# A trunk layer with routed experts: the first gather in one product, four more weight chunks ahead, and a reordered end with row pairs added by GpSimd

## The chip, the cores and the metric

The kernel runs on one core of one Trainium2 chip. The metric is device time in microseconds (us), the median of several executions. A profile is one further execution, recorded instruction by instruction. Engine names as the profile has them: PE is TensorE's matmul, PEld its weight load, DVE is VectorE, ACT is ScalarE, POOL is GpSimd, and SP is SyncE, which here only issues transfers (SPq in the rows).

## The reference, cut to what matters

One layer over 512 tokens of 1024 channels, all in float32. An attention part (two branches, gates, an output projection, a LayerNorm) makes `h`. Then each token picks one group of experts and two experts in that group:

```python
x = _layer_norm(ALPHA * x + mixed, ln1_g, ln1_b)          # h, 512 x 1024
g_val, g_idx = lax.top_k(softmax(x @ w_group + b_group), 1)
top_val, top_idx = lax.top_k(e_logits_of_that_group, 2)
combine = ...                                               # weight of each token in each of 32 experts
for g in range(4):                                          # 8 experts of width 256 in each group
    hid = silu(x @ w_gate[g]) * (x @ w_up[g]) * combine[:, g]
    y = y + hid @ w_down[g]
return _layer_norm(ALPHA * x + y, ln2_g, ln2_b)
```

## The kernel before

**Stages.** Up to about 345 us the kernel projects and attends; to 401 us it multiplies by the output matrix, tile by tile (four tiles of 128 tokens, two halves of 512 columns), adds the residual into `hp[tt]`, normalizes and routes; to 420 us it gathers the rows of the first four experts; then come 32 experts, and from about 646 us on the closing sums, the second LayerNorm and the output.

**Precision.** Exact float32 products are made in two ways: a float32 operand in one product, or a rounded part (type fp32r) and the remainder in two quicker products. `split` makes the two parts: ACT rounds, and DVE or POOL subtracts. `split_h` (line 837) does so for the normalized tile: DVE scales and shifts each half of `hp[tt]` (line 848), ACT writes `hh` (line 112), POOL writes `hl` (line 115), and then the tile goes to DRAM (`hD<-hp`, line 853), from where later experts fetch their rows by index.

**First gather.** The rows of experts 0 to 3 (64 each, so 256) are not fetched but multiplied out: `gathered` (line 995) multiplies `hh[tt]` and `hl[tt]` by a one-hot matrix `onehot` (256 columns) for each of 8 channel blocks and 4 tiles, into eight banks called `trf`. What can be done while the last tiles are routed is done there (table `TAIL`, with some idle products between); tile 3, and blocks 6 and 7, come last, in `prep_first`. `onehot` of tile 3 stands at the end of DVE's routing chain (lines 894 to 929).

**Weights.** The experts' 192 chunks (`we`, 128 x 1024 floats, 512 KB each) are loaded in a fixed order by SP, which waits in order, instruction by instruction. Chunk i goes into a buffer of one of four pools (`RING`: 0 is `slots`, 1 is `slots2`, 2 `hip`, 3 `lop`), 43 buffers in one round. 13 chunks are loaded from inside the output projection (`EARLY`, `EARLY_AT`), five of them into `slots2`; all others are issued from the experts' loop, up to 47 ahead of use, when a buffer comes free. `slots2` has 15 buffers, and also holds `hp`, `hh`, `hl` and the first LayerNorm's gain and bias.

**Experts.** For each expert: `gate_up` (4 chunks, 16 products into `sc`), ACT and DVE join the two half sums into `gus`, four transposes (`stp`), ACT's silu and DVE's multiply (`sg`), then `down` (2 chunks, 8 products into `tr`). For experts 0 to 27 the weighted rows go to DRAM by index (`y2D`), two rows for each token. The last four experts ("late") don't: their rows are kept in SBUF as `late`, split in halves of columns into a rounded and a remainder part (lines 1199, 1204, 1206), and are added into the result by products with a selection matrix `stl`.

**The end.** The two stored rows of every token come back as `yy` (eight transfers of 512 KB, line 1251). Eight banks `fin0` to `fin7` (two for each tile) sum up: products of `late` with `stl` ("add") and products of `yy` with the identity ("rows"). Tiles 0 and 1 take both rows of a pair by products; for tiles 2 and 3 POOL adds the pair first (line 1290). The order is written out by hand in `FIN`. Then statistics, gain, scale and bias of each tile, on DVE, ACT and POOL, and the store.

Of the kernel before, what the change touches and what calls it, by code (L numbers as in the profile page):

```python
# [45 lines left out]
EARLY = 13  # L46
K2 = 5
EARLY_AT = (0, 0, 5)
# [20 lines left out]
H_POOL = (0, 1, 2, 3)  # L69
LATE_C = (2, 3)  # L70
H_STT = (0, 1, 2, 3)
# [9 lines left out]
Y_PE = (0, 1)  # L81
Y_POOL = (2, 3)
# [3 lines left out]
FIN_AT = {31: (0, 1, 2, 3)}  # L86
FIN = (
# [16 lines left out]
def trunk(ctx, tc, xT, x, wm, wv, wbr, wout, wr, br, bg, rbx, lnp, lncol, wexp, out):  # L104
# [726 lines left out]
    hh, hl = [None] * TT, [None] * TT  # L831
# [5 lines left out]
    def split_h(tt):  # L837

        r, mean = rs[tt]
        if tt in LATE_C:  # L840
            centre(tt, mean)
        t = slot([P, D], F32R, f"hh{tt}", slots2)
        lo = slot([P, D], F32R, f"hl{tt}", slots2)
        for k in range(2):
            cs = slice(k * S, (k + 1) * S)
            src = hp[tt][:, cs]
            if tt in H_STT:
                nc.vector.scalar_tensor_tensor(out=src, in0=src, scalar=r, in1=lnb[:, cs], op0=OP.mult, op1=OP.add)
# [197 lines left out]
    for tt in range(TT):  # L1046
        at = (0, tt + 1) if tt + 1 < TT else (1, 0)
        todo.setdefault((*at, PT[0]), []).extend([lambda tt=tt: turn(tt, 0), lambda tt=tt: first_half(tt)])
        todo.setdefault((*at, PT[1]), []).append(lambda tt=tt: run(lg[tt, 0]))
        todo.setdefault((1, tt + 1, PT[0]), []).extend([lambda tt=tt: turn(tt, 1), lambda tt=tt: begin(tt), lambda tt=tt: scale1(tt)])  # L1050
        todo.setdefault((1, tt + 1, PT[1]), []).extend([lambda tt=tt: choose(tt)])
        todo.setdefault((1, tt + 1 + PT[2] // 8, PT[2] % 8), []).append(lambda tt=tt: run(rt[tt]))
        todo.setdefault((1, tt + 1 + PT[3] // 8, PT[3] % 8), []).append(lambda tt=tt: split_h(tt))
# [18 lines left out]
    def load_early():  # L1072
        for _ in range(EARLY):
            raw_load()

    todo.setdefault(EARLY_AT, []).append(load_early)
# [102 lines left out]
    def down(e):  # L1179
        p, odd = e // 2, e % 2  # L1180
        is_late = p >= NPAIR - NLATE
        odd_last = p == NPAIR - 1
        if is_late:
            late.append(hip.tile([P, D], F32R, tag="hi", name=f"late{e}"))
        elif not odd:
            oe[p] = bp.tile([P, D], F32, tag="oe", name="oe", bufs=2)
        ps = pb.tile([P, 512], F32, tag="tr", name="tr", bufs=3)
        sides = [slice(half * CAP, (half + 1) * CAP) for half in range(2)]
# [4 lines left out]
        if is_late:  # L1193
            sums = slot([P, D], F32, f"sum{e}", slots2)
            cs = [slice(half * 512, half * 512 + 512) for half in range(2)]
            scs = [(wslot if half == odd else wswap)[sides[half], p : p + 1] for half in range(2)]
            for half, here in enumerate(sides):
                x = (xg if half == odd else xo)[p]
                pin(nc.vector.scalar_tensor_tensor(
                    out=sums[here, cs[half]], in0=ps[here], scalar=scs[half], in1=x[here, cs[half]],  # L1200
                    op0=OP.mult, op1=OP.add,
                ))
            for half, here in enumerate(sides):
                pin(nc.scalar.activation(late[-1][here, cs[half]], sums[here, cs[half]], AF.Copy))
            for half, here in enumerate(sides):
                pin((nc.gpsimd if half and odd_last else nc.vector).tensor_sub(
                    late[-1][sides[1 - half], cs[half]], sums[here, cs[half]], late[-1][here, cs[half]].bitcast(F32)
                ))
            return
        for half in (odd, 1 - odd):  # L1210
            cs = slice(half * 512, half * 512 + 512)
# [21 lines left out]
    late = []  # L1233
# [51 lines left out]

    def fin_sum(tt):
        a, b = y2[tt]
        if tt in Y_PE:
            return
        pin((nc.gpsimd if tt in Y_POOL else nc.vector).tensor_add(a, a, b))  # L1290

    def finish():

        for step in FIN:
# [3 lines left out]
            if what == "down":  # L1298
                down(tt)
# [4 lines left out]
            elif what == "sum":  # L1304
                fin_sum(tt)
            elif what == "rows":
                for n, t in enumerate(y2[tt] if tt in Y_PE else y2[tt][:1]):
                    fin_rows(tt, t, n == 1 or tt not in Y_PE)
# [42 lines left out]
    for e in range(NE):  # L1351
# [18 lines left out]
        act(e)  # L1370
# [131 lines left out]
```

## Time and profile before

| what | value |
|---|---|
| median of 3 executions | 679.63 us (677.06 to 679.9) |
| the profiled execution: its own time; the span of its instructions | 682.24 us; 680.4 us |
| PE busy; DVE; ACT; POOL | 640.9 us (94%); 408.2 us (60%); 322.6 us (47%); 105.1 us (15%) |
| transfers | 158.62 MB, mean 233 GB/s |
| mean granted clock of TensorE | 0.987 of full speed |

The page begins with the busy time of each engine; a busy PE is not PE at its peak, since products overlap. Then the span is cut in 40 slices of 17 us, each digit a share in tenths. The chain is followed back from the last instruction to what released each step. The views by stretch and by time used below give the same for chosen microseconds.

### The profile page before, as it was taken

What the parts mean: (1) busy time and instruction counts of PE and PEld (TensorE: products, weight loads), DVE (VectorE), ACT (ScalarE), POOL (GpSimd) and SP (SyncE); (2) the same over time, 40 slices, a digit from 0 to 9 for tenths busy, and PEclk for the clock granted to TensorE, in tenths of its full rate; (3) what the DMA queues carried; (4) which work ended last, traced back from release to release, by engine and by line L of the source; (5) the groups of instructions that cost most, each with busy time, mean ns of one, the idle gap of its engine ahead of it and who ended that gap; (6) DMA issues with size and microseconds to landing.
All of it is one profiled execution on the core that took longest, in us unless ns stands there. A gap on an engine that the chain in (4) does not pass through costs nothing.

```text
span 680.4 us, 8940 instructions
## 1 busy us (share of the span) xinstructions
PE 640.9 (94%) x3116; PEld 420.4 (62%) x3116; DVE 408.2 (60%) x836; ACT 322.6 (47%) x642; POOL 105.1 (15%) x152
## 2 busy tenths in 40 slices
PE   8999999999999999989999997899999988889894
PEld 4888878887878888878888775334343322224342
DVE  5676768678868877563674796234444433335466
ACT  5576877766656555744533232333322222222444
POOL 2012121101100110050000133121121111110044
PEclk8999999999999999999999998999999999999997
DMA  8600059203130323016794678999999999999943
GB/s 328 261 0 1 1 191 380 78 2 94 47 108 17 109 78 108 32 57 209 279 362 157 214 252 341 408 408 410 409 408 409 407 408 406 406 403 406 405 198 126
DMA packets 48032, 158.62 MB, mean 233 GB/s; under 512 B 7529, under 2 KB 7673, under 8 KB 47984
## 3 DMA queue, kind: packets, MB, share of 16 engines
q1 hardware_dynamic: 43632, 150.16, 58.2%
q0 software_dynamic: 4352, 7.85, 3.0%
q8 instruction: 26, 0.43, 0.3%
q14 instruction: 22, 0.18, 0.1%
HBM read 150.16 MB, written 15.73 MB: 244 GB/s over the span
## 4 chain that ended last, share of the span: by engine, by line
PE 52%; DMA 20%; DVE 15%; ACT 7%; issue 3%; POOL 0%; SPq 0%; DVEq 0%; POOLq 0%; ACTq 0%
DMA we<-in_wexp_dram 18%; PE pj L130 16%; PE sc L130 10%; PE pb L130 7%; PE po L130 4%; PE tr L130 4%; DVE t L482 3%; PE fin L130 2%; PE pv L130 2%; DVE wl L115 2%; PE av L130 2%; ACT wh L112 2%; DVE t L480 1%; PE tr L536 1%; DMA raw<-in_wm_dram 1%
## 5 line engine op out<-in xcount | busy, mean ns | idle before, releaser
L130 PE MATMUL sc<-we,xp 128*64 128x512 f32 x448 | 108.1, 604 | 7.4 <-DMA we<-in_wexp_dram 5.6
L130 PE MATMUL pj<-xh,wh 128*128 128x512 f32 x256 | 103.9, 406 | 1.7 <-ACT wh L112 1.6
L130 PE MATMUL pj<-xh,wl 128*128 128x512 f32 x256 | 101.2, 395 | 0.0
L130 PE MATMUL pj<-xl,wh 128*128 128x512 f32 x256 | 101.0, 394 | 0.0
L115 DVE TENSOR_TENSOR wl<-raw,wh 128x1024 fp32r<-128x1024 f32 (+1 forms) x57 | 69.9, 1230 | 23.0 <-ACT wh L112 22.8
L1152 DVE TENSOR_TENSOR gus<-gus,sc 64x512 f32<-64x512 f32 x32 | 21.7, 679 | 85.6 <-ACT gus L1151 83.5
L130 PE MATMUL tr<-we,sg 128*64 128x512 f32 x256 | 63.3, 601 | 5.3 <-DMA we<-in_wexp_dram 2.6
L112 ACT ACTIVATE wh<-raw 128x1024 fp32r<-128x1024 f32 (+1 forms) x57 | 58.7, 1037 | 18.7 <-DMA raw<-in_wbr_dram 4.7
L130 PEld LDWEIGHTS sc<-we,xp 128*64 128x64 f32 x448 | 27.4, 136 | 63.2 <-issue 33.1
L1151 ACT ACTIVATE gus<-sc 64x512 f32<-64x512 f32 x32 | 19.0, 593 | 88.6 <-PE sc L130 88.6
L130 PEld LDWEIGHTS pj<-xh,wh 128*128 128x128 f32 x256 | 48.6, 190 | 11.2 <-ACT wh L112 2.1
L130 PEld LDWEIGHTS pj<-xh,wl 128*128 128x128 f32 x256 | 48.5, 189 | 11.1 <-DVE wl L115 0.4
L130 PEld LDWEIGHTS pj<-xl,wh 128*128 128x128 f32 x256 | 48.6, 190 | 8.4
L130 PEld LDWEIGHTS tr<-we,sg 128*64 128x64 f32 x256 | 16.4, 136 | 44.9 <-issue 31.5
L130 PE MATMUL pb<-y,wh 128*128 128x512 f32 x128 | 40.0, 394 | 0.3 <-DVE k L345 0.3
L115 DVE TENSOR_TENSOR wl<-tr,wh 128x512 fp32r<-128x512 f32 (+1 forms) x64 | 30.9, 484 | 11.9 <-ACT wh L112 11.6
L1225 POOL DMA_INDIRECT y2D<-oe,rowi x14 | 14.0, 998 | 146.3 <-DVE oe L1216 120.2
L489 POOL TENSOR_SCALAR_AFFINE_SELECT w<-w 128x128 f32<-128x128 f32 x32 | 16.1, 514 | 126.2 <-ACT w L486 118.5
L112 ACT ACTIVATE wh<-tr 128x512 fp32r<-128x512 f32 (+1 forms) x64 | 27.2, 427 | 12.7 <-PE tr L536 12.4
L1214 ACT ACTIVATE oe<-tr,wswap 64x512 f32<-64x512 f32 x28 | 19.1, 682 | 26.0 <-DVE oe L1218 25.7
L130 PE MATMUL sc<-k,q 128*128 128x512 f32 (+3 forms) x128 | 28.5, 323 | 0.2
L1218 DVE SCALAR_TENSOR_TENSOR oe<-tr,wslot,xg 64x512 f32<-64x512 f32 x24 | 18.0, 750 | 17.0 <-PE tr L130 17.0
(229 smaller groups left out, 1218.9 us busy)
## 6 DMA issues: line engine op xcount, KB each, us to landing
we<-in_wexp_dram SPq DMA_DIRECT2D x192, 512.0 KB
raw<-in_wm_dram SPq DMA_DIRECT2D x32, 512.0 KB
raw<-in_wv_dram SPq DMA_DIRECT2D x8, 512.0 KB
y2D<-zero SPq DMA_DIRECT2D x16, 256.0 KB
raw<-in_wbr_dram SPq DMA_DIRECT2D x8, 512.0 KB
raw<-in_wout_dram SPq DMA_DIRECT2D x8, 512.0 KB
yy<-y2D SPq DMA_DIRECT2D x8, 512.0 KB
strip<-in_rbx_dram SPq DMA_DIRECT2D x8, 256.0 KB
```

The lines of the kernel that those rows point to most:

```text
L112: act = nc.scalar.activation(hi, src, AF.Copy)
L115: pin((eng or nc.vector).tensor_sub(lo, src, hi.bitcast(F32)), fix == "both")
L130: pin(nc.tensor.matmul(ps, a, b, start=start, stop=stop))
L480: nc.vector.scalar_tensor_tensor(out=t, in0=ps, scalar=0.0, in1=t, op0=OP.max, op1=OP.add)
L482: nc.vector.tensor_tensor_scan(out=t[:, ::-1], data0=t[:, ::-1], data1=mk[:, ::-1], initial=0.0, op0=OP.add, op1=OP.mult)
L489: nc.gpsimd.affine_select(out=blk, in_=blk, pattern=[[-1, P]], compare_op=OP.is_gt, fill=0.0, base=0, channel_multiplier=1)
L536: nc.tensor.transpose(tr[:, i * P : (i + 1) * P], w[:, off + j * P : off + (j + 1) * P], ident)
L1151: pin(nc.scalar.activation(gus[e], ps[CAP:], AF.Copy))
L1152: pin(nc.vector.tensor_add(gus[e], gus[e], ps[:CAP]))
L1214: nc.scalar.activation(dst, ps[here], AF.Copy, scale=(wslot if half == odd else wswap)[here, p : p + 1])
L1218: nc.vector.scalar_tensor_tensor(out=dst, in0=ps[here], scalar=wslot[here, p : p + 1], in1=xg[p][here, cs], op0=OP.mult, op1=OP.add)
L1225: nc.gpsimd.indirect_dma_start(out=y2D[:, :], out_offset=bass.IndirectOffsetOnAxis(ap=rowi[:, p : p + 1], axis=0), in_=oe[p], in_offset=No ...
```

## The change

Three edits in one kernel.

1. `split_h` becomes `norm_h`: DVE's scale and shift, and the store to DRAM, stay; ACT's rounding and POOL's subtraction go, with the eight `hh` and `hl` buffers. `gathered` multiplies `hp[tt]` itself by `onehot`, both read as float32: 32 float32 products instead of 64 fp32r products.
2. `EARLY` loads 13 chunks where it did, and 4 more at step (0, 3, 5), inside the first half of tile 3's projection. `K2` goes from 5 to 9, so that chunks 13 to 16 go into `slots2`, and every later chunk up to 42 into the place that the chunk four before it had.
3. At the end, the late experts' steps are taken apart and written in `FIN` one by one (prod: products; rows, high, low: lines 1199, 1204, 1206), expert 31's silu stands before the roundings of expert 29, the table load comes after them, only one remainder is left to POOL (`S_POOL`), banks 0 to 3 are opened at expert 30 instead of 31, and POOL adds all four row pairs ("pair"), each bank then taking one product ("yrow").

```diff
-EARLY = 13
-K2 = 5
-EARLY_AT = (0, 0, 5)
+EARLY = (13, 4)
+K2 = 9
+EARLY_AT = ((0, 0, 5), (0, 3, 5))
...
-Y_PE = (0, 1)
-Y_POOL = (2, 3)
-FIN_AT = {31: (0, 1, 2, 3)}
+FIN_AT = {30: (0, 1, 2, 3)}
+S_POOL = ((30, 1),)
...
 FIN = (
-    "down30 down31 add0.2 add1.2 add2.2 add3.2 rows0 sum2 sum3 add0.3 add1.3 add0.4 add1.4 stat0.0 "
...
+    "prod29 stp31 silu31 rows29.0 gate31 rows29.1 high29.0 high29.1 table0 low29.0 "
+    "prod30 rows30.0 rows30.1 high30.0 high30.1 low29.1 pair0 prod31 rows31.0 rows31.1 high31.0 high31.1 "
+    "low30.0 low30.1 low31.0 low31.1 pair1 pair2 pair3 "
...
-    def split_h(tt):
+    def norm_h(tt):
...
-        t = slot([P, D], F32R, f"hh{tt}", slots2)
-        lo = slot([P, D], F32R, f"hl{tt}", slots2)
         for k in range(2):
...
-            split(t[:, cs], lo[:, cs], src, eng=nc.gpsimd if tt in H_POOL else None, fix=tt in H_STT)
+            held[1] = nc.vector.scalar_tensor_tensor(
+                out=src, in0=src, scalar=r, in1=lnb[:, cs], op0=OP.mult, op1=OP.add
+            )
         nc.sync.dma_start(hD[tt * P : (tt + 1) * P, :], hp[tt])
...
     def gathered(ps, c, ts):
         for tt in ts:
-            for n, h in enumerate((hh, hl)):
-                mm(
-                    ps, h[tt][:, c * P : (c + 1) * P], onehot[:, tt, :],
-                    tt == 0 and n == 0, tt == TT - 1 and n == 1,
-                )
+            mm(ps, hp[tt][:, c * P : (c + 1) * P], onehot[:, tt, :].bitcast(F32), tt == 0, tt == TT - 1)
...
+    def late_low(e, half):
+        here, cs = sides[half], halves[half]
+        pin((nc.gpsimd if (e, half) in S_POOL else nc.vector).tensor_sub(
+            late[e][sides[1 - half], cs], sums[e][here, cs], late[e][here, cs].bitcast(F32)
+        ))
...
     def fin_sum(tt):
         a, b = y2[tt]
-        if tt in Y_PE:
-            return
-        pin((nc.gpsimd if tt in Y_POOL else nc.vector).tensor_add(a, a, b))
+        pin(nc.gpsimd.tensor_add(a, a, b))
```

What stands in SP's row of transfers behind the last chunks of the output matrix (`raw54`, `raw55`), before; the names in brackets are what an instruction waits for (DMAHW: an earlier transfer).

```order
L178 DMA raw55_3587<-in_wout_dram 128x1024 [waits DMAHW2_49,DVE_49,Activation_49]
L1069 DMA we13_4039<-in_wexp_dram 128x1024 [waits DMAHW3_49,DVE_49]
L1069 DMA we14_4041<-in_wexp_dram 128x1024 [waits DMAHW4_49,DVE_49]
L1069 DMA we15_4043<-in_wexp_dram 128x1024 [waits DMAHW5_49,DMAHW1_49,DVE_49]
L1069 DMA we16_4045<-in_wexp_dram 128x1024 [waits DMAHW6_49,DMAHW2_49,DVE_49]
L1069 DMA we17_4047<-in_wexp_dram 128x1024 [waits DMAHW7_49,PE_49]
L1069 DMA we18_4049<-in_wexp_dram 128x1024 [waits DMAHW0_49,PE_49]
L853 DMA hD_61<-hp0_3400 128x1024 [waits DVE_49]
L1069 DMA we19_4051<-in_wexp_dram 128x1024 [waits PE_49]
```

The same place in the changed kernel:

```order
L179 DMA raw55_3587<-in_wout_dram 128x1024 [waits DMAHW2_49,DVE_49,Activation_49]
L1059 DMA we13_3602<-in_wexp_dram 128x1024 [waits DMAHW3_49]
L1059 DMA we14_3604<-in_wexp_dram 128x1024 [waits DMAHW4_49]
L1059 DMA we15_3606<-in_wexp_dram 128x1024 [waits DMAHW5_49]
L1059 DMA we16_3608<-in_wexp_dram 128x1024 [waits DMAHW6_49,DVE_49]
L1059 DMA we17_3991<-in_wexp_dram 128x1024 [waits DMAHW7_49,DVE_49]
L1059 DMA we18_3993<-in_wexp_dram 128x1024 [waits DMAHW0_49,DVE_49]
L1059 DMA we19_3995<-in_wexp_dram 128x1024 [waits DMAHW1_49,DVE_49]
L1059 DMA we20_3997<-in_wexp_dram 128x1024 [waits DMAHW2_49,DVE_49]
L1059 DMA we21_3999<-in_wexp_dram 128x1024 [waits DMAHW3_49,PE_49]
L1059 DMA we22_4001<-in_wexp_dram 128x1024 [waits DMAHW4_49,PE_49]
```

Before, chunk 13 waits for DVE; now chunks 13 to 15 wait for earlier transfers alone, and the store of tile 0 (`hD<-hp0`) has chunk 22 in front of it where it had chunk 18.

Further on in SP's row, from the store of tile 3 on; before:

```order
L853 DMA hD_61<-hp3_3403 128x1024 [waits DMAHW5_49,DVE_49]
L1069 DMA we28_4069<-in_wexp_dram 128x1024 [waits DMAHW6_49]
L1069 DMA we29_4071<-in_wexp_dram 128x1024 [waits DMAHW7_49]
L1069 DMA we30_4073<-in_wexp_dram 128x1024 [waits DMAHW0_49]
L1069 DMA we31_4075<-in_wexp_dram 128x1024 [waits DMAHW1_49]
L1069 DMA we32_4077<-in_wexp_dram 128x1024 [waits DMAHW2_49]
L1069 DMA we33_4079<-in_wexp_dram 128x1024 [waits DMAHW3_49]
L1069 DMA we34_4081<-in_wexp_dram 128x1024 [waits DMAHW4_49,DMAHW5_49,PE_49,Pool_49]
L1069 DMA we35_4083<-in_wexp_dram 128x1024 [waits PE_49]
L1069 DMA we36_4085<-in_wexp_dram 128x1024 [waits DMAHW6_49,PE_49]
L1069 DMA we37_4087<-in_wexp_dram 128x1024 [waits DMAHW7_49,PE_49]
```

and in the changed kernel:

```order
L848 DMA hD_61<-hp3_3403 128x1024 [waits DMAHW1_49,DVE_49]
L1059 DMA we32_4021<-in_wexp_dram 128x1024 [waits DMAHW2_49]
L1059 DMA we33_4023<-in_wexp_dram 128x1024 [waits DMAHW3_49]
L1059 DMA we34_4025<-in_wexp_dram 128x1024 [waits DMAHW4_49]
L1059 DMA we35_4027<-in_wexp_dram 128x1024 [waits DMAHW5_49]
L1059 DMA we36_4029<-in_wexp_dram 128x1024 [waits DMAHW6_49]
L1059 DMA we37_4031<-in_wexp_dram 128x1024 [waits DMAHW7_49]
L1059 DMA we38_4033<-in_wexp_dram 128x1024 [waits DMAHW0_49]
L1059 DMA we39_4035<-in_wexp_dram 128x1024 [waits DMAHW1_49,PE_49]
L1059 DMA we40_4037<-in_wexp_dram 128x1024 [waits DMAHW2_49,PE_49]
L1059 DMA we41_4039<-in_wexp_dram 128x1024 [waits DMAHW3_49,PE_49]
```

Here the first chunk behind the store is 28 before and 32 now. The first that waits for PE is the seventh behind it before (chunk 34) and the eighth now (chunk 39); chunks 39 to 42 take the places of the four `hp` tiles.

The end of POOL's row, before (behind the last store of rows into `y2D`):

```order
L1206 TENSOR_TENSOR late30_5732<-sum30_5738,late30_5732 64x512
L1206 TENSOR_TENSOR late31_5745<-sum31_5751,late31_5745 64x512
L1290 TENSOR_TENSOR yy20_5613<-yy20_5613,yy21_5614 128x1024
L1290 TENSOR_TENSOR yy30_5617<-yy30_5617,yy31_5618 128x1024
L1347 TENSOR_TENSOR res0_5772<-res0_5772,gb21_5564 128x512 x2
```

and in the changed kernel:

```order
L1298 TENSOR_TENSOR yy00_5549<-yy00_5549,yy01_5550 128x1024
L1208 TENSOR_TENSOR late30_5675<-sum30_5681,late30_5675 64x512
L1298 TENSOR_TENSOR yy10_5553<-yy10_5553,yy11_5554 128x1024
L1298 TENSOR_TENSOR yy20_5557<-yy20_5557,yy21_5558 128x1024
L1298 TENSOR_TENSOR yy30_5561<-yy30_5561,yy31_5562 128x1024
L1358 TENSOR_TENSOR res0_5716<-res0_5716,gb21_5508 128x512 x2
```

POOL has four pair sums instead of two, the first of them ahead of its remainder, and one remainder less, which DVE takes over.

## Rows read from the trace of the kernel before

**Rows 1.** The page: span, transfers in 40 slices, the chain by line

```profile
span 680.4 us, 8940 instructions
...
DMA  8600059203130323016794678999999999999943
...
DMA we<-in_wexp_dram 18%; PE pj L130 16%; PE sc L130 10%; PE pb L130 7%; PE po L130 4%; PE tr L130 4%; DVE t L482 3%; PE fin L130 2%; PE pv L130 2%; DVE wl L115 2%; PE av L130 2%; ACT wh L112 2%; DVE t L480 1%; PE tr L536 1%; DMA raw<-in_wm_dram 1%
```

**Rows 2.** Stretches: us, busy of five engines, PEclk, DMA share, GB/s

```profile
354.00:368.00 14.00, 14.00 (x75) 11.74 (x74) 3.30 (x5) 2.55 (x5) 0.00 (x0) 1.00 0.52 210
...
402.00:411.00 9.00, 6.30 (x48) 5.61 (x48) 8.96 (x33) 2.80 (x6) 2.64 (x2) 0.97 0.81 284
411.00:425.00 14.00, 11.85 (x71) 8.89 (x71) 8.93 (x33) 3.39 (x10) 4.39 (x13) 0.90 0.99 375
...
440.00:520.00 80.00, 79.25 (x410) 30.42 (x410) 32.23 (x53) 25.56 (x48) 13.81 (x14) 1.00 1.03 409
520.00:600.00 80.00, 72.41 (x342) 22.80 (x338) 29.46 (x49) 20.20 (x39) 10.48 (x11) 1.00 1.03 407
```

**Rows 3.** SP's transfers in order of time: start, us, count

```profile
352.44 1.61 SPq L178 DMA_DIRECT2D raw<-in_wout_dram  x2
368.72 10.52 SPq L1069 DMA_DIRECT2D we<-in_wexp_dram  x6
...
410.42 0.33 SPq L853 DMA_DIRECT2D hD<-hp  x1
```

**Rows 4.** What SP waited for, 300 to 650 us: total, times, longest

```profile
SPq L1069 <- DVE wl L115: 18.3, 4, 13.7
...
SPq L1069 <- PE trf L130: 5.2, 2, 4.8
```

**Rows 5.** DVE and POOL, 402 to 412 us, in order of time

```profile
402.57 1.28 POOL L115 TENSOR_TENSOR hl<-hp,hh 128x512 fp32r<-128x512 f32 x1 [1.29 <-ACT hh L112]
...
402.88 1.00 DVE L899 TENSOR_TENSOR small_xe<-small_xe 128x4 f32<-128x4 f32 x1
...
404.40 0.17 DVE L901 SCALAR_TENSOR_TENSOR small_xe<-small_xe,small_oe 128x32 f32<-128x32 f32 x1
...
406.94 0.74 DVE L848 SCALAR_TENSOR_TENSOR hp<-hp,small_xe,lnb 128x512 f32<-128x512 f32 x1
...
408.48 1.36 POOL L115 TENSOR_TENSOR hl<-hp,hh 128x512 fp32r<-128x512 f32 x1 [4.63 <-ACT hh L112]
...
408.71 1.68 DVE L848 SCALAR_TENSOR_TENSOR hp<-hp,small_xe,lnb 128x512 f32<-128x512 f32 x1
...
410.97 0.16 DVE L899 TENSOR_TENSOR small_xe<-small_xe 128x4 f32<-128x4 f32 x1
...
411.17 1.29 DVE L901 SCALAR_TENSOR_TENSOR small_xe<-small_xe,small_oe 128x32 f32<-128x32 f32 x1
```

**Rows 6.** The chain in order of time: fast gather products, the closing sums

```profile
417.28 2.87 PE trf L130 x22
...
654.36 16.98 PE fin L130 x52
```

**Rows 7.** Float32 products of 512 columns, in order of time

```profile
660.13 3.60 PE L130 MATMUL fin<-yy,ident 128*128 128x512 f32 x8
```

**Rows 8.** The end, in order of time

```profile
651.29 0.28 ACT L1161 ACTIVATE sg<-stp 128x128 f32<-128x128 f32 x1
...
652.42 1.94 PE L130 MATMUL tr<-we,sg 128*64 128x512 f32 x8 [1.14 <-DVE sg L1165]
...
654.56 0.74 DVE L1199 SCALAR_TENSOR_TENSOR sum<-tr,wswap,xo 64x512 f32<-64x512 f32 x1
654.61 1.28 POOL L1206 TENSOR_TENSOR late<-sum,late 64x512 fp32r<-64x512 f32 x1 [23.47 <-ACT late L1204]
...
658.16 4.69 POOL L1290 TENSOR_TENSOR yy<-yy,yy 128x1024 f32<-128x1024 f32 x2
```

**Rows 9.** Stretches of the end, columns as in rows 2

```profile
658.00:660.00 2.00, 2.00 (x9) 1.31 (x8) 0.36 (x1) 0.00 (x0) 1.92 (x2) 1.00 0.04 14
```

More of the change, by code (lines that the diff above doesn't have):

```diff
@@ L1070, in raw_load, with load_early @@
         raw_e.append(t)
[L1072 to L1073 removed]
+    def load_early(n):
+        for _ in range(n):
             raw_load()
[L1076 removed]
+    for at, n in zip(EARLY_AT, EARLY):
+        todo.setdefault(at, []).append(lambda n=n: load_early(n))
     for half in range(2):
@@ L1177, in late_x, with down_mm @@
         pin(nc.scalar.activation(xo[p][a, :S], xg[p][b, :S], AF.Copy))
[L1179 to L1186, printed above, removed]
+    sides = [slice(half * CAP, (half + 1) * CAP) for half in range(2)]
+    halves = [slice(half * 512, half * 512 + 512) for half in range(2)]
+    late, psl, sums = {}, {}, {}
+    def down_mm(e):
         ps = pb.tile([P, 512], F32, tag="tr", name="tr", bufs=3)
-        sides = [slice(half * CAP, (half + 1) * CAP) for half in range(2)]
         for f in range(2):
@@ L1192, in down @@
                 mm(ps[sides[half]], hid[e][:, f, :], w[:, half * 512 : half * 512 + 512], f == 0, f == 1)
[L1193 to L1208, printed above, removed]
+        return ps
@@ new lines, in late_mm, with late_rows @@
+    def late_mm(e):
+        late[e] = hip.tile([P, D], F32R, tag="hi", name=f"late{e}")
+        psl[e] = down_mm(e)
+        sums[e] = slot([P, D], F32, f"sum{e}", slots2)
+    def late_rows(e, half):
+        p, own = e // 2, half == e % 2
+        here, cs = sides[half], halves[half]
+        pin(nc.vector.scalar_tensor_tensor(
+            out=sums[e][here, cs], in0=psl[e][here], scalar=(wslot if own else wswap)[here, p : p + 1],
+            in1=(xg if own else xo)[p][here, cs], op0=OP.mult, op1=OP.add,
+        ))
@@ new lines, in late_high, with down @@
+    def late_high(e, half):
+        here, cs = sides[half], halves[half]
+        pin(nc.scalar.activation(late[e][here, cs], sums[e][here, cs], AF.Copy))
+    def late_low(e, half):
+        here, cs = sides[half], halves[half]
+        pin((nc.gpsimd if (e, half) in S_POOL else nc.vector).tensor_sub(
+            late[e][sides[1 - half], cs], sums[e][here, cs], late[e][here, cs].bitcast(F32)
+        ))
+    def down(e):
+        p, odd = e // 2, e % 2
+        if p >= NPAIR - NLATE:
+            late_mm(e)
+            for part in (late_rows, late_high, late_low):
+                for half in range(2):
+                    part(e, half)
@@ L1209, in down @@
             return
+        if not odd:
+            oe[p] = bp.tile([P, D], F32, tag="oe", name="oe", bufs=2)
+        ps = down_mm(e)
         for half in (odd, 1 - odd):
-            cs = slice(half * 512, half * 512 + 512)
+            cs = halves[half]
             here, dst = sides[half], oe[p][sides[odd], cs]
@@ L1297, in finish @@
             cols = [slice(k * S, k * S + S) for k in range(2)]
-            if what == "down":
-                down(tt)
+            if what in ("prod", "stp", "silu", "gate"):
+                dict(prod=late_mm, stp=act_t, silu=act_s, gate=act_g)[what](tt)
+            elif what[:-2] in ("rows", "high", "low"):
+                dict(rows=late_rows, high=late_high, low=late_low)[what[:-2]](int(what[-2:]), tt)
+            elif what == "table":
+                tc.keep_in_program_order(nc.scalar.preload_act_table_set("natural_log_exp_and_others"))
             elif what == "open":
@@ L1303, in finish @@
                 fin_add(int(what[3:]), tt)
-            elif what == "sum":
+            elif what == "pair":
                 fin_sum(tt)
-            elif what == "rows":
-                for n, t in enumerate(y2[tt] if tt in Y_PE else y2[tt][:1]):
-                    fin_rows(tt, t, n == 1 or tt not in Y_PE)
+            elif what == "yrow":
+                fin_rows(tt)
             elif what == "stat0":
```

52 lines of the change are left out of this document (21 added, 31 removed), and 5 rows, old and new, of the table FIN.

## The prediction

> **What bounds the kernel now.** I read the page first, then the stretches, then SP's row of transfers, and last the end in order of time. The page's chain names the weight transfers as its largest part, 18%, and the slices show transfers at nine tenths or more from the 25th slice almost to the end [rows 1]. The stretches say where that begins: from 411 us on the DMA share is at 0.99 and above, 409 and 407 GB/s from 440 to 600; PE is full until 520 (79.25 of 80 us) and falls to 72.41 of 80 behind that, where it waits for chunks [rows 2]. So there are three stages with three limits: up to 411 us transfers have room (share 0.52 from 354 to 368, 0.81 from 402 to 411); from 411 to about 650 us everything hangs on how early the transfers began to run without a gap; and behind the last chunk there is an end of some 30 us on PE, DVE and POOL. What the change gives in the middle is read from SP's row: how many chunks have gone through when the gapless stretch starts.
>
> One chunk is 512 KB, 524,288 bytes; at 409 GB/s [rows 2] that is 1.28 us. All sums below are against the profiled execution: span 680.4 us [rows 1], its own time 682.24, so 1.84 us lie around the span. That execution is 2.61 us above the median of 679.63; I scale by the ratio at the end.
>
> **Four chunks ahead.** SP stands still for 13.7 us, the longest wait of its kind [rows 4]: between the last two output-weight transfers at 352.44 and chunk 13 at 368.72 [rows 3], which waits for DVE to free a buffer. In the changed order chunks 13 to 16 stand there with only transfers in front of them (16 also waits for DVE, for a gate tile consumed before this stretch). The stretch has 14 us at 210 of 409 GB/s [rows 2], so room for 14 x 199,000 = 2.8 MB; four chunks are 2.1 MB. They cost nothing there, PE is full with products whose weights have been issued before. Every later chunk then takes the buffer that the one four before it had, and at tile 3's store chunks up to 31 have gone instead of 27. The value is 4 x 1.28 = 5.1 us off every landing in the gapless stretch. Bounds: 0 if the later buffers come free too late, 5.1.
>
> **The split that goes.** ACT and POOL lose eight instructions each, which were not the bound. But while POOL subtracts, DVE instructions with two SBUF inputs stand: the same L899 takes 1.00 us beside POOL and 0.16 alone, L848 1.68 and 0.74, L901 1.29 and 0.17 [rows 5]. DVE is the full engine of 402 to 411 us, 8.96 of 9 [rows 2]. L899 and L848 lie before tile 3's store at 410.42 [rows 3]: 0.84 + 0.94 = 1.8 us earlier; L901 lies behind it, on the way to the last `onehot`: 1.1 us more. The transfers can use of this only what they have idle: 9 us at a share of 0.81 against 1.03 [rows 2] is 9 x 0.21 = 1.9 us. Bounds 0 to -1.8; I take -1.3.
>
> **The gather in float32.** The eight records of 3.60 us are four float32 products of 512 columns, one every 0.86 us with the drain of the last taken off [rows 7]; 256 columns are half, 0.43. Two fp32r products took 2 x 2.87 / 22 = 0.26 us [rows 6]. 32 products cost 32 x 0.17 = 5.4 us more on PE, most of it inside waits for `onehot` (PE has 6.30 of 9 us in 402 to 411). Behind the last `onehot` stand 11: 4.7 us for 2.87, +1.9. The last `onehot` itself comes up to 1.8 + 1.1 = 2.9 us earlier by DVE, but PE's six products of tile 2 and the idle products stand ahead of its routing product: six at 0.17 more take 1 us of that back. Net the gather ends about where it did, 420.1 us.
>
> That matters for transfers in a new way: chunks 39 to 42 now take the `hp` tiles themselves, and wait for the end of the gather, with all of SP's row behind them. Before, a like wait (4.8 us, for `trf` [rows 4]) was covered: seven chunks had been issued behind the store, and the share stayed at 0.99 [rows 2]. Now too seven are issued, but the store is 1.3 us earlier, so the queue runs dry that much sooner. I cost it at +0.4 us; bounds 0, and +7 where the products run at half the clock (rival 3). Sum of the stream: -5.1 - 1.3 + 0.4 = -6.0.
>
> **The end.** Two things get shorter. Expert 31's silu ran at 651.29 behind two roundings, and its `down` products waited for it until 652.42 [rows 8]; now it runs ahead of them, and `down` can start at about 649.9, when the products of expert 30 end: -2.5 us on PE. And PE adds eight float32 products into `fin` instead of twelve: -4 x 0.86 = -3.4 [rows 7]. The four `fin` products of expert 28 go into a hole of PE at expert 30, for nothing. The closing products ran from 654.36 for 16.98 us, to 671.3 [rows 6]: twelve float32 at 0.86 and 28 fp32r ones, so 0.24 each. If nothing stopped PE from 654.9 on (the first pair sum, below), eight float32 (6.9 us) and 24 fp32r ones (5.8; the other four run in a wait ahead) would end at 667.6: -3.7.
>
> POOL stands against it. A pair sum is 4.69 / 2 = 2.35 us, a remainder 1.28 [rows 8]; four sums and one remainder are 10.7 us in a row, from the landing of the first pair on. That landing I estimate: eight transfers at 1.28, the last bytes by 660 us [rows 9], so the second at about 652.3. From there to 663 or later POOL reads SBUF without a pause, and DVE has four remainders of two SBUF inputs left to do (late29's second, one of late30, two of late31), on which `fin0` and `fin1` wait. No row of before shows this overlap: DVE's sum beside POOL's remainder reads one of its inputs from a PSUM bank, takes 0.74, and is not held [rows 8]. The nearest rows for two SBUF inputs are L848, L899 and L901 [rows 5], and all three are held until POOL is done, so I let each DVE remainder wait for one POOL instruction: late30's at 654.9, late31's behind POOL's remainder at 656.9 and behind the second pair sum at 660.0, done 660.7. Then six float32 products and 22 fp32r ones are left, 5.2 + 5.3 us: 671.2. Value -0.1; bounds -3.7 (not held) and +3 (the first pair sum gets in ahead of late29's second remainder, +2.35, or PE idles for 3 us there and runs on at a lower clock, as it did in 411 to 425, PEclk 0.90 [rows 2]).
>
> The Trainium skill, page "SBUF — State Buffer", section "SBUF: two separate sides", says of this that DVE with two SBUF inputs and a GpSimd instruction that reads SBUF share an exclusive pair of ports, and whichever starts first keeps it for the whole instruction while the other fully blocks. That agrees with rows 5, speaks for the first edit and against the third; by it the end gives -0.1 or worse, without it -3.7.
>
> **The rivals.** 1. *The end is not held*, or DVE keeps its turn through several remainders: PE runs from 654.9 to 667.6 without a gap, -6.0 - 3.7 = -9.7, 670.0 after scaling; with two kept turns about -8. For it: DVE sums beside POOL are not held in rows 8; against it: rows 5.
> 2. *The end gets longer*: the first pair sum lands before late29's second remainder, everything on DVE is 2.35 us later, PE idles and its clock falls: end +3, total -3, 676.6. For it: 0.4 us between the two in my estimate.
> 3. *Slower than before*: the gather's float32 products run at the lower of the two clock levels (1.2 GHz). In 411 to 425 the granted clock was 0.90 on average [rows 2], after PE had been filled to 6.30 of 9. Then each product is 0.86: the six of tile 2 take 5.2 us, the last eleven 9.5; the gather ends at about 429 us, chunk 39 is issued 9 us late, the queue of 9 us runs dry and the landings come about 3 us later than before: 682.6. It decides from a gather end of about 426 us on; between 420 and 426 the gain shrinks from -6 to 0. Against it: the float32 products fill the holes in which the clock fell.
> 4. *The chunks ahead don't move the stream*, because a later wait swallows them (buffers, order in SP): only edits one and three count, about -1.5: 678.1. Against it: chunks 32 to 38 wait for transfers alone.
>
> **How the numbers follow.** Forecast: 682.24 - 6.1 = 676.1, times 679.63 / 682.24: 673.5. Chances: forecast 0.50 (its own range 671 to 676), rival 1 0.24, rival 2 0.12, rival 3 0.06, rival 4 0.08. The range runs from 668.8 (rival 1, with all of the 1.9 us of idle transfers) to 678 (rivals 2 and 4) and leaves out most of rival 3. A measurement of this kernel tells about 0.5%, 3.4 us, from no change, so faster means below 676.2: forecast 0.47, rival 1 0.24, rival 2 0.05: 0.76. Slower by over 0.5% is above 683: the far half of rival 3 and some of the unknown, 0.05. The rest, 0.19, is same.
>
> **What the profile after would show.** Four chunk transfers between 354 and 360, and a share near 0.75 from 354 to 368; if SP still stands there, rival 4. L848 at 0.75 and L901 at 0.2 throughout, tile 3's store at 408 to 409; if they stay long, the split was not what held them. The first `gate_up` between 419 and 422; from 426 on, rival 3. PE full until about 545 instead of 520. `yy` issued about 6 us earlier; if less, a gap in transfers near 420. At the end: silu ahead of the roundings, DVE remainders of more than 0.7 us beside pair sums, `fin0` full 8 to 10 us behind the landing of the first pair; if they take 0.7 and PE has no gap, rival 1. Most wrong would be a stream that gains under 3 us.

## The result, and the profile after

The changed kernel takes 673.02 us (median of 6 executions, 670.79 to 674.53), the kernel before 679.76 beside it (677.06 to 681.91): a ratio of 0.9873, 95% interval 0.9835 to 0.9911. The forecast was 673.5. The profiled execution took 673.72 us. From the page of the changed kernel, the span and the transfers in 40 slices:

```profile
span 672.0 us, 8900 instructions
...
DMA  8600059202130314015797669999999999999943
```

The long run of nines begins in the 25th slice, a slice earlier than before (there it is the 26th, with an 8 in the 25th [rows 1]). The stretches say more (us, busy of five engines, PEclk, DMA share, GB/s, as in [rows 2]):

```profile
300.00:320.00 20.00, 18.07 (x95) 15.09 (x94) 11.48 (x26) 9.02 (x13) 3.95 (x14) 1.00 0.53 169
...
354.00:368.00 14.00, 14.00 (x75) 11.76 (x74) 4.81 (x6) 3.69 (x7) 0.00 (x0) 1.00 0.73 284
...
402.00:411.00 9.00, 9.00 (x58) 8.15 (x58) 7.93 (x39) 0.63 (x3) 2.91 (x12) 1.00 0.98 375
411.00:425.00 14.00, 12.57 (x60) 6.55 (x59) 3.52 (x9) 3.69 (x7) 0.00 (x0) 1.00 0.98 383
...
520.00:600.00 80.00, 73.82 (x356) 24.41 (x355) 30.01 (x50) 20.73 (x40) 10.11 (x10) 1.00 1.02 403
```

Transfers now fill 0.73 of 354 to 368 (0.52 before) and 0.98 of 402 to 411 (0.81); PE is full in 402 to 411 (6.30 of 9 before) at a clock of 1.00. One stretch differs that no edit touches: 300 to 320. The same view of the kernel before has there, and in a stretch that is needed below,

```profile
300.00:320.00 20.00, 18.07 (x89) 15.17 (x88) 11.78 (x26) 8.69 (x13) 4.53 (x15) 0.91 0.41 125
...
382.00:402.00 20.00, 18.84 (x104) 14.90 (x102) 19.65 (x65) 5.26 (x12) 6.77 (x5) 1.00 0.59 199
```

PE stood for 1.9 us in both and ran on, in the profile of before, at a lower granted clock: everything behind is 2.1 us later there (0.6 of it stood ahead of that wait already), through no part of the change. In the profiles below the time at which this stretch is left differs by up to 6.5 us (321.65 to 328.12), and a median can mix executions of both kinds. So traces are compared from a landmark behind that place, the first transfer of the output weights. SP's transfers of the changed kernel:

```profile
321.75 12.29 SPq L179 DMA_DIRECT2D raw<-in_wout_dram  x4
...
350.98 26.18 SPq L1059 DMA_DIRECT2D we<-in_wexp_dram  x10
...
404.60 0.33 SPq L848 DMA_DIRECT2D hD<-hp  x1
...
632.18 9.13 SPq L1263 DMA_DIRECT2D yy<-y2D  x8
```

and of the kernel before, the first and the last of the same marks:

```profile
323.83 12.29 SPq L178 DMA_DIRECT2D raw<-in_wout_dram  x4
...
640.83 9.17 SPq L1251 DMA_DIRECT2D yy<-y2D  x8
```

From the landmark to the first `yy` the stream takes 632.18 - 321.75 = 310.4 us, before 317.0: -6.6. From there to the span's end it is 672.0 - 632.18 = 39.8, before 39.6: +0.2. Unrounded, -6.57 + 0.25 and the 2.08 ahead make the 8.4 us by which the spans differ. Forecast were -6.0 and -0.1. The following numbers are these two, for each kernel.

### The profile page after: what moved, and what is told of

It reads as the page before. It is cut to its first block, busy times and chain, and to the rows that moved or that the text cites. A ratio compares the mean times of both kernels' runs of the same rounds, so it can differ in the third digit from the quotient of the medians.

```text
span 672.0 us, 8900 instructions
## 1 busy us (share of the span) xinstructions
PE 638.9 (95%) x3108; PEld 421.7 (63%) x3108; DVE 406.7 (61%) x837; ACT 317.3 (47%) x634; POOL 98.8 (15%) x145
## 4 chain that ended last, share of the span: by engine, by line
PE 54%; DMA 26%; DVE 10%; ACT 6%; issue 2%; POOL 0%; SPq 0%; DVEq 0%; POOLq 0%; ACTq 0%
DMA we<-in_wexp_dram 24%; PE pj L131 19%; PE po L131 7%; PE pb L131 7%; PE sc L131 6%; PE trf L131 3%; PE pv L131 3%; PE av L131 2%; DVE t L483 2%; DVE wl L116 2%; PE fin L131 2%; PE tr L537 2%; PE tr L131 2%; DMA raw<-in_wm_dram 2%; ACT wh L113 1%
## 5 line engine op out<-in xcount | busy, mean ns | idle before, releaser
L131 PE MATMUL sc<-we,xp 128*64 128x512 f32 x448 | 106.3, 602 | 4.8 <-DMA we<-in_wexp_dram 3.5
L131 PE MATMUL pb<-y,wh 128*128 128x512 f32 x128 | 40.1, 394 | 0.3 <-DVE k L346 0.3
L537 PE MATMUL tr<-ident,w 128*128 128x128 f32 x160 | 27.9, 272 | 0.0
```

The source lines that it names most:

```text
L131: pin(nc.tensor.matmul(ps, a, b, start=start, stop=stop))
L537: nc.tensor.transpose(tr[:, i * P : (i + 1) * P], w[:, off + j * P : off + (j + 1) * P], ident)
```

## The experiments

Times are medians of all executions; kernels of one group ran on one chip. The kernel before took 680.88 us beside e1 to e4, 680.31 beside e5, e6, e7_pair0_on_pe and after_again, 680.25 beside e7_again and e8. "Stream" is the time from the landmark to the first `yy`, "end" from there to the span's end, both from one profile each.

| kernel | time, us | ratio to before (95%) | stream | end |
|---|---|---|---|---|
| before; changed | 679.76; 673.02 | 0.9873 (0.9835 to 0.9911) | 317.0; 310.4 | 39.6; 39.8 |
| e1_no_ahead | 672.95 | 0.9845 (0.9804 to 0.9885) | 309.7 | 40.0 |
| e2_old_end | 672.60 | 0.9855 (0.9816 to 0.9893) | 308.7 | 39.3 |
| e3_idle_split | 680.48 | 0.9998 (0.9969 to 1.0026) | 316.8 | 39.8 |
| e4_gate | 671.14 | 0.9829 (0.9791 to 0.9867) | 310.2 | 38.0 |
| e5_buffers_kept | 680.13 | 0.9972 (0.9932 to 1.0012) | 313.5 | 40.1 |
| e6_pool_beside | 675.33 | 0.9924 (0.9893 to 0.9955) | 311.8 | 38.4 |
| e7_pair0_on_pe; e7_again | 670.35; 671.00 | 0.9858 (0.9810 to 0.9907); 0.9841 (0.9801 to 0.9881) | 308.8; 308.7 | 37.6; 37.7 |
| after_again | 672.23 | 0.9876 (0.9835 to 0.9917) | 308.9 | 40.0 |
| e8_no_xg_memset | 668.13 | 0.9808 (0.9769 to 0.9848) | 309.2 | 37.7 |

The eight with the changed kernel's stream (the changed kernel, after_again, e1, e2, e4, both e7, e8) lie between 308.7 and 310.4, mean 309.3; that scatter is the measure for the others. Differences of 2 us between medians lie inside the intervals of the ratios (some 0.4% either way); what is said of such differences rests on the traces.

**e1_no_ahead**

```diff
-EARLY = (13, 4)
-K2 = 9
-EARLY_AT = ((0, 0, 5), (0, 3, 5))
+EARLY = (13,)
+K2 = 5
+EARLY_AT = ((0, 0, 5),)
```

> The changed kernel without its second edit: no four chunks ahead (13 chunks early, five of them in slots2). The changed kernel's median is 673.0. Theory A (by the prediction: the stream's head start sets the time, 1.28 us for each chunk, nothing is given back later): 673.0 + 5.1 = 678.1, chunk 13 issued about 366 to 369 us, the last chunk issued 5.1 us later than in the changed kernel, the end as long as there. Rival B (the chunks ahead only fill a stretch that had cover anyway, and the time came from the end): 673.0 to 675, the last chunk less than 2 us later.

Measured: 672.95, no slower than the changed kernel, so beside the first edit the second gives nothing. Theory A fell, and rival B's number came for a reason that it did not give. SP's transfers of this kernel:

```profile
322.18 12.29 SPq L179 DMA_DIRECT2D raw<-in_wout_dram  x4
...
349.27 1.58 SPq L179 DMA_DIRECT2D raw<-in_wout_dram  x2
351.74 25.84 SPq L1059 DMA_DIRECT2D we<-in_wexp_dram  x10
```

Ten chunks follow the output weights at once here too. The order of SP's row shows which (chunk numbers behind `we`):

```
L179 DMA raw55_3587<-in_wout_dram 128x1024 [waits DMAHW2_49,DVE_49,Activation_49]
L1059 DMA we33_4023<-in_wexp_dram 128x1024 [waits DMAHW3_49]
L1059 DMA we34_4025<-in_wexp_dram 128x1024 [waits DMAHW4_49]
L1059 DMA we35_4027<-in_wexp_dram 128x1024 [waits DMAHW5_49]
L1059 DMA we13_3983<-in_wexp_dram 128x1024 [waits DMAHW6_49,DVE_49]
```

Chunks 33 to 35 are the first that `RING` puts into `slots2` behind the early five. With `hh` and `hl` gone that pool has four free buffers (15, less five early chunks, four `hp` and the gain and bias), so they wait for no engine, only for an earlier transfer, and stand at the front (36 follows behind 16). The first edit makes the room; the second only says which chunks use it.

**e2_old_end**, against the changed kernel; `FIN`, `down` and `fin_rows` too are those of before:

```diff
-FIN_AT = {30: (0, 1, 2, 3)}
-S_POOL = ((30, 1),)
+Y_PE = (0, 1)
+Y_POOL = (2, 3)
+FIN_AT = {31: (0, 1, 2, 3)}
```

> The first two edits with the end of the kernel before (old order, row pairs of tiles 0 and 1 by products). Theory A (the end gave nothing, because its gain went to DVE remainders that stand behind POOL's instructions and to PE at a lower clock): 673.0 within 1 us, and the time from the first yy issue to the end of the span as in the kernel before, within 0.5 us. Rival B (the end gave what its count of products promises, 3.7 us): 676.7.

Measured: 672.60, end 39.3. Theory A held, B fell: the new end gives nothing, by the trace it costs half a microsecond.

**e3_idle_split**, against e1_no_ahead:

```diff
+        t = slot([P, D], F32R, f"hh{tt}", slots2)
+        lo = slot([P, D], F32R, f"hl{tt}", slots2)
...
+            split(t[:, cs], lo[:, cs], src, eng=nc.gpsimd, fix=True)
```

> As the kernel without chunks ahead, but ACT's rounding and POOL's subtraction of each tile run as before, and nobody reads what they write (the gather still multiplies hp in float32). So against e1_no_ahead only the split is back. Theory A (POOL's subtraction holds DVE's instructions with two SBUF inputs): scale-and-shift and onehot instructions take 1.0 to 1.7 and 1.3 us beside POOL, tile 3's store comes 2 to 3.7 us later, the first gate_up about 4 us later, and the time is 1.3 us above e1_no_ahead (0 to 1.9): about 679.4. Rival C (the hold is hidden, the early gather end came from the float32 products): same time as e1_no_ahead, gather end unchanged.

Measured: 680.48, which is 7.5 above e1_no_ahead where 1.3 was expected, and the time of the kernel before. Theory A had the direction and missed the size; rival C fell. SP's transfers:

```profile
322.03 12.29 SPq L179 DMA_DIRECT2D raw<-in_wout_dram  x4
...
366.90 10.51 SPq L1062 DMA_DIRECT2D we<-in_wexp_dram  x6
...
408.67 0.33 SPq L851 DMA_DIRECT2D hD<-hp  x1
```

Two things are back: the hole behind the output weights, though nothing of the second edit was touched (the edit takes the eight tiles from `slots2` again, which the expectation had overlooked), and tile 3's store 3.8 us late. The store's lateness is gathered over several tiles; at tile 1, in order of time:

```profile
390.16 1.41 POOL L116 TENSOR_TENSOR hl<-hp,hh 128x512 fp32r<-128x512 f32 x1 [5.57 <-ACT hh L113]
...
390.50 1.62 DVE L847 SCALAR_TENSOR_TENSOR hp<-hp,small_xe,lnb 128x512 f32<-128x512 f32 x1
```

The next two runs take the buffers and the hold apart.

**e5_buffers_kept**, against e3_idle_split:

```diff
-            split(t[:, cs], lo[:, cs], src, eng=nc.gpsimd, fix=True)
+            if k == 1:
+                nc.scalar.activation(t[:, :1], src[:, :1], AF.Copy)
+                nc.scalar.activation(lo[:, :1], src[:, :1], AF.Copy)
```

> As the kernel without chunks ahead (672.95), but the eight hh and hl tiles are taken from slots2 again as in the kernel with the idle split (680.48): ACT writes one column of each, and nothing else of the split runs, so POOL subtracts nothing. Theory E (two separate gains of the first edit: the buffers that hh and hl no longer take, and POOL's hold on DVE): chunk 13 waits to about 367 us again, five transfers less before 402 us, but scale-and-shift and onehot instructions are short; 672.95 + 4 x 1.28 = 678.1, the other 2.4 us of the difference of 7.5 being the hold. Rival F (the hold is all of it, the buffers are worth nothing): 673. Rival G (the buffers are all of it): 680.5.

Its median mixes: six of its twelve executions took 675.0 to 678.4 us and six 681.9 to 683.5; the profiled one shows the granted clock at 0.66 in 300 to 320. By the median alone rival G (680.5) would stand; from the landmark on the trace can be read:

```profile
328.12 12.29 SPq L179 DMA_DIRECT2D raw<-in_wout_dram  x4
...
372.95 10.51 SPq L1064 DMA_DIRECT2D we<-in_wexp_dram  x6
...
410.90 0.33 SPq L853 DMA_DIRECT2D hD<-hp  x1
...
641.64 9.23 SPq L1268 DMA_DIRECT2D yy<-y2D  x8
```

Chunk 13 waits again (44.8 us behind the landmark, as 44.9 in e3_idle_split and 29.2 in the changed kernel), but tile 3's store stands at 82.8, where the changed kernel has 82.9 and e3_idle_split 86.6. The stream is 313.5: the buffers alone are worth 313.5 - 309.3 = 4.2 us, and the hold the 316.8 - 313.5 = 3.3 that are left to e3_idle_split. Theory E held; F and G fell.

**e6_pool_beside**, against the changed kernel (`idle` is a scratch that nobody reads):

```diff
+            nc.gpsimd.tensor_sub(idle, src, lnb[:, cs])
```

> The changed kernel, with one POOL subtraction of 128x512 behind each of DVE's scale-and-shift instructions, into a scratch that nobody reads; no buffer is taken for it. Theory E: the hold alone is back, DVE's instructions with two SBUF inputs are long again, tile 3's store 2 to 4 us later than in the changed kernel, the four chunks ahead stay: 673.0 + 2.4 = 675.4. Rival F: 680. Rival G: 673.0.

Measured: 675.33 where 675.4 was expected. SP's transfers:

```profile
323.16 12.29 SPq L179 DMA_DIRECT2D raw<-in_wout_dram  x4
...
353.25 25.30 SPq L1061 DMA_DIRECT2D we<-in_wexp_dram  x10
...
409.14 0.33 SPq L849 DMA_DIRECT2D hD<-hp  x1
...
634.93 9.24 SPq L1265 DMA_DIRECT2D yy<-y2D  x8
```

The chunks are ahead, the store is late (86.0 behind the landmark), the stream 311.8: the hold alone costs 311.8 - 309.3 = 2.5 us. Beside 3.3 by the other way, the hold is 2.5 to 3.3. Which DVE instruction is held depends on when POOL starts. Here the scale and shift keeps its 0.73 to 0.75, and another instruction with two SBUF inputs, 0.25 in the changed kernel (its line 882), lasts until POOL is done:

```profile
406.50 1.27 POOL L848 TENSOR_TENSOR small_xe<-hp,lnb 128x512 f32<-128x512 f32 x1 [3.98 <-DVE hp L845]
...
406.58 1.25 DVE L884 SCALAR_TENSOR_TENSOR small_xe<-small_xe 128x40 f32<-128x40 f32 x1
```

**e4_gate**, against the changed kernel:

```diff
-S_POOL = ((30, 1),)
+S_POOL = ()
-    "low30.0 low30.1 low31.0 low31.1 pair1 pair2 pair3 "
+    "low30.0 low30.1 low31.0 low31.1 after0 pair1 pair2 pair3 "
+            elif what == "after":
+                gate = bp.tile([P, 1], F32, tag="gate", name="gate", bufs=1)
+                pin(nc.gpsimd.tensor_copy(gate, late[31][:, 512:513].bitcast(F32)))
```

> The changed kernel, but all remainders of the late experts by DVE, and POOL copies one column of the last remainder before its second pair sum, so that it waits until DVE is done. Theory A (the end's gain was lost because each DVE remainder stood behind one POOL instruction): low30.0 waits for the first pair sum (646.3 in the changed kernel's trace), then four remainders of 0.69 in a row, done 649.1 instead of 651.25; second pair sum at 651.6 instead of 650.6; fin0 full 2 us earlier, PE without the drop of its clock, time 673.0 - 2.0 = 671.0 (670 to 671.7). Rival D (the end hangs on the landing of the rows or on PE's own products): 673.0, or 0.6 more because pair sums come later.

The end of the changed kernel first, in order of time:

```profile
639.68 0.28 ACT L1156 ACTIVATE sg<-stp 128x128 f32<-128x128 f32 x1 [1.50 <-PE stp L1152]
...
643.79 2.48 POOL L1298 TENSOR_TENSOR yy<-yy,yy 128x1024 f32<-128x1024 f32 x1 [21.16 <-DMA yy<-y2D]
...
645.64 5.61 DVE L1208 TENSOR_TENSOR late<-sum,late 64x512 fp32r<-64x512 f32 x3
...
648.02 7.77 POOL L1298 TENSOR_TENSOR yy<-yy,yy 128x1024 f32<-128x1024 f32 x3
...
651.31 2.50 PE L131 MATMUL fin<-late,stl 128*128 128x512 f32 x5 [2.26 <-DVE late L1208]
```

Three DVE remainders, 0.69 each when nothing stands beside them, take 5.61 us beside POOL. Silu runs early, as meant, and PE then waits 2.26 us for the last remainder. Its clock falls as well, in the stretches:

```profile
651.00:654.50 3.50, 3.19 (x7) 2.19 (x8) 3.25 (x7) 1.23 (x6) 3.50 (x2) 0.52 0.00 0
```

With the gate:

```profile
646.65 3.57 DVE L1208 TENSOR_TENSOR late<-sum,late 64x512 fp32r<-64x512 f32 x4
...
649.00 2.71 PE L131 MATMUL fin<-late,stl 128*128 128x512 f32 x8
```

Four remainders in 3.57 us, PE without the long stop, and the end is 38.0 instead of 39.8 to 40.1: -1.8 to -2.0, as theory A had it. 671.14 us is 1.8 below e1_no_ahead of the same group, no more than the medians' noise; the trace is what speaks against rival D.

That part of the loss was the clock, e6_pool_beside shows by chance. Its remainders take as long (5.72 us), but its first two `yy` products already ran at the lower clock, while PE had to wait anyway, and the clock is back when PE needs it. Stretches, then PE in order of time:

```profile
648.00:654.00 6.00, 4.29 (x7) 1.90 (x7) 5.94 (x4) 0.78 (x2) 5.84 (x4) 0.72 0.16 66
654.00:657.50 3.50, 3.42 (x11) 2.19 (x12) 3.40 (x8) 1.68 (x7) 3.50 (x2) 1.00 0.00 0
```

```profile
654.08 1.43 PE L131 MATMUL fin<-late,stl 128*128 128x512 f32 x5 [0.70 <-DVE late L1210]
```

1.43 us for what takes 2.50 above; its end is 38.4, 1.4 us shorter than the changed kernel's with the same code. By this comparison the greater part of the gate's 1.8 to 2.0 us is the clock that PE keeps.

**e7_pair0_on_pe**, against e4_gate:

```diff
-    "prod30 rows30.0 rows30.1 high30.0 high30.1 low29.1 pair0 prod31 rows31.0 rows31.1 high31.0 high31.1 "
+    "prod30 rows30.0 rows30.1 high30.0 high30.1 low29.1 prod31 rows31.0 rows31.1 high31.0 high31.1 "
...
     def fin_rows(n):
+        if n < 2:
+            mm(fin[n], ident, y2[0][1][:, halves[n]], False, False)
```

> The kernel with the gate, and besides the first row pair is added by PE products (two float32 products more) instead of POOL, so that POOL does nothing before DVE's last remainder. By the hold: four remainders in 2.8 us, done 0.8 us earlier than with the gate, the two products more lie in PE's wait for them (1.5 us with the gate): 2.7 us below the changed kernel, 0.7 below the gate. Rival (PE's order: the products more than fill the wait and push the rest): 1 us above the gate's time.

```profile
645.44 3.60 PE L131 MATMUL fin<-yy,ident 128*128 128x512 f32 x8
646.18 2.84 DVE L1208 TENSOR_TENSOR late<-sum,late 64x512 fp32r<-64x512 f32 x4
```

With no POOL beside them, four remainders take 2.84 us, and PE's two additional products lie where it waited. The end is 37.6, -0.4 to the gate (0.7 expected); 670.35 us is 1.9 below the changed kernel run beside it, which was to be 2.7.

**after_again** and **e7_again** are repeats, for comparison on one chip.

> The changed kernel once more, on the chip of these runs, to compare the others with: 0.987 of the kernel before.

> The kernel with the gate and the first row pair on PE once more, to compare with on this chip: 0.985 of the kernel before.

Both came as expected within their intervals (0.9876 and 0.9841).

**e8_no_xg_memset**, against e7_pair0_on_pe:

```diff
-    for t in xgb:
-        nc.gpsimd.memset(t, 0.0)
...
         nc.sync.dma_start(hD[tt * P : (tt + 1) * P, :], hp[tt])
+        if tt < XGB:
+            nc.scalar.activation(xgb[tt], hp[tt], AF.Copy, scale=0.0)
```

> The kernel with the gate and the first row pair on PE, and one change far from the end: the three xg tiles are set to zero by ACT (copies of normalized tiles at scale 0, one behind each of the first three tiles' normalization) instead of by POOL at 299.4 to 302.1 us. In all traces so far two DVE copies of 128x128 take 5.18 us there beside POOL's MEMSETs, PE then stands 1.9 us (302 to 303.9) for DVE, and in some executions runs on at the lower clock. Theory H (POOL's MEMSETs hold these DVE copies as its subtractions hold the others): the copies end at about 299.9 instead of 302.6, PE's wait falls from 1.9 to about 0.5 us, the clock in 300 to 320 stays at 1.00, and the time is 1.5 us lower where the clock did not fall, 2 to 4 us over the mean of executions: about 667 to 669 beside 670.4. Rival (the copies wait for something else): the copies still end at 302.6, the time is the same.

The changed kernel, DVE and POOL at that place:

```profile
297.39 5.18 DVE L1274 COPY bc<-lnc 128x128 f32<-128x128 f32 x2
...
299.39 2.74 POOL L719 MEMSET xg<- 128x1024 f32 x3
...
303.89 0.68 PE L131 MATMUL psb<-small_xe 128*128 128x40 f32 x4 [1.93 <-DVE small_xe L692]
```

Without the three MEMSETs:

```profile
297.18 2.49 DVE L1274 COPY bc<-lnc 128x128 f32<-128x128 f32 x2
...
299.32 0.20 POOL L721 MEMSET small_oe<- 128x128 bf16 x1
```

(the copies still wait here, for other MEMSETs that stay: they end at 299.67, 0.15 us behind the last of these) and its stretch, where PE has no gap and keeps its clock:

```profile
300.00:320.00 20.00, 20.00 (x106) 17.10 (x105) 8.68 (x24) 9.73 (x15) 1.05 (x7) 1.00 0.66 226
```

Theory H held: 668.13 us, 2.9 below the same kernel with the MEMSETs beside it, and its six executions lie within 1.1 us (667.68 to 668.77), where the twelve of after_again reach from 668.9 to 679.6. This is the best version: 0.9808 of the kernel before.

## Why the prediction was right, point by point

The time was right, in part by luck: the mechanisms are there, but one of the stream's terms stood on the wrong edit, two were too small, and the errors cancel in part. 5.1 + 1.3 - 0.4 = 6.0 was forecast; 4.2 for the buffers (with the gather's wait in it) and 2.5 to 3.3 for the hold were measured, 6.7 to 7.5, both from the first edit; the first two profiles differ by 6.6.

- **Four chunks ahead, -5.1.** The mechanism stands: chunk transfers begin behind the output weights, and the head start stays to the end of the stream. It measured 4.2, for four chunks of 1.28 us, 5.1; most of what is missing was lost again at the gather (below). The step that failed is the one that gave it to the second edit. "Chunks 13 to 16 stand there with only transfers in front of them" is true of the changed order, but e1_no_ahead, without that edit, has ten chunks in the same place. The room in `slots2` was made by taking out `hh` and `hl`. Rival 4, by which edits one and three alone would be worth 1.5, fell with it: they are worth all of it. Whether the second edit could stand without the first was not tried.
- **The split that goes, -1.3, bounds 0 to -1.8.** 2.5 to 3.3, outside the bounds. The step that failed is the bound "9 us at a share of 0.81": I let the transfers use only what they had idle between 402 and 411, and counted only the two instructions that I saw held there (L899, still of tile 2, and L848 of tile 3). But POOL's subtractions held DVE at tiles 1 and 2 as well (1.62 us in the row of e3_idle_split, 1.70 at the next tile). From the landmark the stores of tiles 1, 2 and 3 come 1.1, 2.0 and 3.8 us earlier in e1_no_ahead than in e3_idle_split, and transfers had room from 382 on (share 0.59 before, the row above). The sign for the mechanism was right. DVE in the changed kernel, in order of time:

```profile
403.84 0.73 DVE L845 SCALAR_TENSOR_TENSOR hp<-hp,small_xe,lnb 128x512 f32<-128x512 f32 x1
...
405.35 0.19 DVE L895 SCALAR_TENSOR_TENSOR small_xe<-small_xe,small_oe 128x32 f32<-128x32 f32 x1
```

  These are lines 848 and 901 of before, which took 1.68 and 1.29 beside POOL [rows 5].
- **The gather in float32, +0.4.** Too small. The products do what was forecast: from the landmark the first `gate_up` starts at 96.3 us before, at 98.4 in e3_idle_split (float32 products, hold kept) and at 94.5 in e1_no_ahead (hold gone). So the products cost 2.1 us (1.9 forecast) and the end of the hold gives 3.9 back (up to 2.9 forecast). But the term prices another thing, the wait of chunks 39 to 42 for the end of the gather. SP stood 5.5 us for it in the changed kernel (total, times, longest, 330 to 440 us), 1.3 in e3_idle_split, and behind the seven chunks the transfers thinned out, as the stretch 415 to 421 shows:

```profile
SPq L1059 <- PE trf L131: 5.9, 2, 5.5
```

```profile
415.00:421.00 6.00, 4.84 (x22) 1.82 (x20) 0.89 (x2) 1.07 (x2) 0.00 (x0) 1.00 0.91 337
```

  337 of 409 GB/s [rows 2] for 6 us is 6 x (1 - 337 / 409) = 1.1 us, an estimate from this trace. e5_buffers_kept, against which the four chunks were measured, moved 412 GB/s in the like stretch (421 to 427): 5.1 less 1.1 is 4.0, and 4.2 was measured. No run takes this wait away by itself. The clock was 1.00 in 411 to 425, and rival 3 fell.
- **The end, -0.1.** Near in number (+0.2), and held as forecast, but the number is in part luck. Each remainder stood for one POOL instruction; by the rows shown with e4_gate the last one was done 7.5 us behind the start of the first pair sum (643.79 to 651.25), where the forecast had 8.4 (652.3 to 660.7). The clock of 0.52 in 651 to 654.5, which I had only as a bound, took that back and more: e6_pool_beside, held as long but at a clock of 1.00 from 654 on, has an end of 38.4, which is 1.2 below before. Rival 1 (the end is not held) is what e7_pair0_on_pe makes true by removing what holds: 37.6 against 39.6 before, -2.0 of the 3.7 promised, with two float32 products more on PE than the rival had.
- **Signs.** PE is busy 73.82 of 80 us in 520 to 600 (72.41 before), and `yy` was issued 8.65 us earlier, 6.6 without the execution's own 2.1; the forecast said about 6. Tile 3's store (404.6) and the first `gate_up` (416.3) came ahead of the forecast 408 to 409 and 419 to 422, also with the 2.1 added: the hold was larger than I had it.

## What to carry to other kernels

A buffer that an edit frees is a head start for every transfer that waits for a place in that pool, so price an edit by the tiles it drops as well as by the instructions; then ask whether a second edit "that loads ahead" adds anything to it. Beside a busy POOL, count DVE's instructions with two SBUF inputs by POOL's durations, and for all tiles through which the delay adds up. Where only order is wrong, a POOL instruction that reads one column of DVE's last output is a cheap way to let DVE go first.

## What the runs showed of the hardware that was not expected

A DVE COPY of 128x128 with a single SBUF input is held by POOL's MEMSETs, which read nothing, and not for one of them: the two copies in the changed kernel took 5.18 us, got no turn between the MEMSETs, and ended at 302.57, 0.15 us behind the last of the row, as in e8_no_xg_memset. The remainders at the end got a turn after each POOL instruction. A subtraction of 128x512 with two SBUF inputs beside a MEMSET of the same row took 0.69 us, as alone (the eight of its kind take 0.69 to 0.70):

```profile
295.65 3.64 POOL L633 MEMSET small_xe<- 128x1024 f32 x4
...
296.78 0.69 DVE L116 TENSOR_TENSOR y<-yr,y 128x512 fp32r<-128x512 f32 x1 [1.15 <-ACT y L113]
...
302.22 0.20 POOL L723 MEMSET small_oe<- 128x128 bf16 x1
```

The Trainium skill, page "SBUF — State Buffer", section "SBUF: two separate sides", says that DVE's two-port forms (a float32 copy within SBUF is its example) and any GpSimd instruction exclude each other, and two SBUF inputs only count against a GpSimd instruction that reads SBUF. The traces agree with both halves: 5.18 us for the copies, 0.69 for the subtraction beside MEMSETs, 5.61 for three subtractions beside sums.

The same wait of PE, 1.9 us at 302 us in eleven profiles of equal code up to there, was followed by three different granted clocks in 300 to 320: 1.00, 0.91 and 0.66, with the landmark at 321.7 to 322.2, 322.8 to 324.1 and 327.8 to 328.1 us. That is 6 us between profiles of the same instructions, nearly as much as the whole change is worth, from a gap that MEMSETs ahead of it had made: without three of them (e8_no_xg_memset) the gap is gone and the clock stays at 1.00. What decides between the three is not shown.
